# A hybrid transformer block on one core: the first modulation as fp32 matmuls in column quarters, and a written order around the first weight sums

## The chip, the cores and the metric

The kernel runs on one core of one Trainium2 chip, as one launch. Its time is device time in microseconds (us). Before the change three runs took 698.64, 700.24 and 700.47 us, with 700.24 us as their median. Five engines work side by side, each with its own queue, strictly in the order of its own instructions: PE (TensorE; its weight loads are listed as PEld), DVE (VectorE), ACT (ScalarE), POOL (GpSimd) and SP (SyncE, which here issues all transfers).

## The reference

The input x has 512 tokens of 1024 values. A vector c gives six modulation vectors, the first two of which (shift and scale) act on the first normalization. All arithmetic is fp32:

```
mod = silu(c) @ w_ada + b_ada                    # w_ada: 1024 x 6144
sh1, sc1, g1, sh2, sc2, g2 = split(mod, 6)
hn  = rms(x, norm1_g) * (1 + sc1) + sh1
y   = mixer(hn, w_in, ...)                       # three kinds of attention heads
x   = x + g1 * (y @ w_out)
hn  = rms(x, norm2_g) * (1 + sc2) + sh2
gate, up = split(hn @ w_gate_up, 2)
x   = x + g2 * ((silu(gate) * up) @ w_down)
```

The change touches two places: how sh1 and sc1 (2 x 1024 numbers, from 8 MB of w_ada) are made in the first stage, and the order of DVE and ACT where the gated part of the block (gate, up) begins.

## The kernel before, in words

**First stage.** It makes the transposed, modulated operand `hnT` (eight pieces `kc` of 128 features by 512 tokens) and, with it, one 512-column product of `w_in`, summed over the eight pieces in the four banks `gT`. Every fp32 operand of a large matmul is split into a rounded high part and the low rest (names end in h and l), and a product is three matmuls: high by high, low by high, high by low. So a step `kc` needs:

- `px_` (line 320): four 128 x 128 transposes of the scaled x on PE.
- The two modulation columns of these 128 features. w_ada lies as 8 rows k per partition; `asc` holds the scale columns and `ash` the shift columns of the piece, each 128 x 8 x 128. `scaled` (333) sums the eight rows of `asc`, times silu(c) (`cs`), on DVE into `a1`. `product` (325) multiplies six rows of `ash` on ACT and `addto` (329) sums them on POOL into `a2`; `direct` (340) multiplies the last two on PE. `colsum` (346) then sums over partitions: two matmuls with a column of ones put scale and shift as columns into `pc`. In the trace `a1` and `a2` are both called a.
- `m1_` (351, DVE) adds the constants, `hf_` (358, ACT) applies scale and shift to the transposed x, `hh_` (363) and `hl_` (369, DVE) split the result.
- `wh_` (372, ACT) and `wl_` (376, POOL) split the piece of `w_in`, and `T_` (380) does its twelve 512-column matmuls.

Before that x is squared, a reciprocal root `rs` is made by eleven tiny DVE instructions, and x is scaled (`xscale`, 300). All of these are entered with a time into a table (`ev`, 297) whose constants (PER = 3.5 us for a step, and so on) decide the order; line 423 writes them out sorted by time, and `_InOrder` (105) holds every engine to that order in this stage. The w_ada piece 0 is loaded before x.

**Where the gated part begins.** `plain(0)` and `plain(1)` (1247) are plain products of the first two column blocks for the two halves of the tokens; `plain_glu` (1264) takes their result: ACT makes `fps` = silu(gate), DVE multiplies it with up into `A`. After them the products are made by a scheme with sums of weights and operands: `sums` (1144) adds raw weight blocks r on DVE (r1t is the first such sum), ACT and DVE split it into fw16h and fw16l, and PE needs these for its first product f1A after `plain(1)`. `operand` (1073) splits operand sums (os40 among them). Temporary tiles, `fps` among them, come from `temp` (1130), a ring of 26 slots (`act_tile`, 226) that also lends a pair named sph, spl to the weights of `plain(1)`: `spare("act")` in line 1213. Here no order is imposed on DVE and ACT (line 432 has switched it off): a scheduler orders them.

Of the kernel before, what the change touches and what calls it, by code (L numbers as in the profile page):

```python
# [28 lines left out]
SHK = 6  # L29
# [102 lines left out]
def hybrid_block_kernel(  # L132
# [22 lines left out]
    def f32(ap):  # L155
        return ap.bitcast(F32)
# [103 lines left out]
    with ExitStack() as s0:  # L260
# [7 lines left out]
        for kc in range(NK):  # L268
            box["asc", kc] = ap_.tile([P, 8, P], F32, tag="asc", name=f"asc{kc}", bufs=3)
            box["ash", kc] = ap_.tile([P, 8, P], F32, tag="ash", name=f"ash{kc}", bufs=3)  # L270

        def load_ada(kc):
            SY.dma_start(box["asc", kc], w_ada_v[:, :, D + kc * P:D + kc * P + P])
            SY.dma_start(box["ash", kc], w_ada_v[:, :, kc * P:kc * P + P])

        if ADA1ST:
            load_ada(0)
# [4 lines left out]
        if not ADA1ST:  # L282
            load_ada(0)
# [11 lines left out]
        plan = []  # L295

        def ev(time, f, *a, **k):
            plan.append((time, len(plan), lambda: f(*a, **k)))

# [6 lines left out]
        for t in range(NT - 1):  # L306
            ev(XQ + 0.01 * t, square, t, slice(0, D), ss[:, t:t + 1] if t % 2 else "S")
        ssx = cp.tile([P, 1], F32, name="ssx")
        ev(XQ + 0.03, square, NT - 1, slice(0, D // 2), "S")
        ev(XQ + 0.03, square, NT - 1, slice(D // 2, D), ssx)  # L310
        ev(XQ + 0.04, V.tensor_tensor, ss[:, NT - 1:NT], ss[:, NT - 1:NT], ssx, op=ALU.add)
        ev(XR, V.tensor_scalar, v1, ss, 1.0 / D, EPS, op0=ALU.mult, op1=ALU.add)
        for i, f in enumerate(rsqrt_ops(rs, v1, "n4")):
            ev(XR + XRD * (i + 1), f)
# [10 lines left out]
        def product(kc, k):  # L325
            ash, a2 = box["ash", kc], box["a2", kc]
            S.activation(a2 if k == 0 else ash[:, k, :], ash[:, k, :], AF.Copy, scale=cs[:, k:k + 1])

        def addto(kc, k):
            ash, a2 = box["ash", kc], box["a2", kc]  # L330
            G.tensor_tensor(a2, a2, ash[:, k, :], op=ALU.add)

        def scaled(kc, k):
            asc, a1 = box["asc", kc], box["a1", kc]
            if k == 0:
                V.tensor_scalar(a1, asc[:, 0, :], cs[:, 0:1], None, op0=ALU.mult)
            else:
                V.scalar_tensor_tensor(a1, asc[:, k, :], cs[:, k:k + 1], a1, op0=ALU.mult, op1=ALU.add)

        def direct(kc):  # L340
            pc = box["pc", kc] = bank("t", f"pc{kc}")
            ash = box["ash", kc]
            for k in range(SHK, 8):
                TE.matmul(pc[:, 1:2], ash[:, k, :], cs[:, k:k + 1], start=k == SHK, stop=False)

        def colsum(kc):
            pc = box["pc", kc]
            TE.matmul(pc[:, 1:2], box["a2", kc], ones[:, 0:1], start=SHK == 8, stop=True)
            TE.matmul(pc[:, 0:1], box["a1", kc], ones[:, 0:1], start=True, stop=True)

        def m1_(kc):
            pc = box["pc", kc]
            m1 = box["m1", kc] = ap_.tile([P, 2], F32, tag="m1", name=f"m1{kc}")
            V.scalar_tensor_tensor(m1[:, 0:1], pc[:, 0:1], b1sc[:, 0, kc:kc + 1],
                                   prmT[:, 48 + kc:49 + kc], op0=ALU.add, op1=ALU.mult)
            V.tensor_tensor(m1[:, 1:2], pc[:, 1:2], prmT[:, kc:kc + 1], op=ALU.add)
# [31 lines left out]
        for kc in range(NK):  # L390
            box["a1", kc] = ap_.tile([P, P], F32, tag="a1", name=f"a1{kc}")
            box["a2", kc] = ap_.tile([P, P], F32, tag="a2", name=f"a2{kc}")
            ws = box["ws", kc] = wp.tile([P, 512], F32, tag="ws", name=f"w0s{kc}", bufs=WS)
            b_ = kc * PER
            if kc:
                ev(b_ - 9, load_ada, kc)
            ev(b_ - 9, SY.dma_start, ws, w_in[0, kc * P:(kc + 1) * P, MQK:MQK + 512])
            for k in range(8):
                ev(b_ + 0.39 * k, scaled, kc, k)
                if k < SHK:  # L400
                    ev(b_ + 0.3 * k, product, kc, k)
                    if k:
                        ev(b_ + 0.5 * k + 0.3, addto, kc, k)
            ev(b_ + TWH if kc or not ADA1ST else XQ + 0.035, wh_, kc)
            ev(b_ + TWL, wl_, kc)
            tx = max(b_ + TPX, XR + 13 * XRD, max(XT, XR + 12.5 * XRD) + XD + 0.1 if kc * P >= XS else 0)
            tc_ = b_ + TPC if kc else TPC0
            tm = tc_ + TM1 if kc else TPC0 + TM10
            th = max(tm + THF, tx + 0.1)
            ev(tx, px_, kc)  # L410
            ev(tc_, direct, kc)
            ev(tc_, colsum, kc)
            ev(tm, m1_, kc)
            ev(th, hf_, kc)
            ev(max(tm + THH, th + 0.05), hh_, kc)
            tl = max(tm + THL, th + THH - THF + 0.1)
            ev(tl, hl_, kc)
            ev(max(b_ + TPC + PER, tl) + 0.1, T_, kc)

        for i in range(NWARM):  # L420
            ev(WARM0 + WARM1 * i, TE.matmul, gT[3][:, 0:256], ident,
               box["ws", 0][:, 0:256], start=True, stop=True)
        for _, _, f in sorted(plan, key=lambda e: e[:2]):
            f()
# [875 lines left out]
    plain_glu(0)  # L1300

# [27 lines left out]
    for i, (q, ph) in enumerate(run):  # L1329
        upto = todo.index(run[min(i + AHEAD, len(run) - 1)])  # L1330
        while ahead <= upto:
            prepare(*todo[ahead])
            if todo[ahead] == (NQ - 1, 1):
                down_load(4)
            if todo[ahead] == (1, 6):
                for g_ in range(2):
                    operand("s4", g_, s4[g_])
                plain_glu(1)
            ahead += 1
        product(q, ph)  # L1340
        after(q, ph)
# [72 lines left out]
```

## Time and profile before

| | |
|---|---|
| median of three runs | 700.24 us |
| the profiled execution, its own time | 700.27 us |
| its span, first to last instruction | 698.5 us |
| PE busy | 655.9 us, 94% |
| DVE busy | 546.1 us, 78% |
| ACT busy | 370.4 us, 53% |
| POOL busy | 133.7 us, 19% |
| mean granted clock of PE | 0.98 of full |

The profile comes from one execution. Busy shares are means over stages with different limits; for a change in one stage one reads the waits and the chain of that stage. Between the span and the execution's own time lie 1.8 us in which no instruction runs. PE's clock is either at full (2.4 GHz, 1.00 in the rows) or half (1.2 GHz, 0.50); a value between is a mean over a stretch.

### The profile page before, as it was taken

The page shows a single profiled execution, that of the slowest core. Times are in us where ns is not written, and L with a number is a line of the kernel's source. Part 1 is how long each engine was busy: PE and PEld are TensorE (multiplying, and loading weights), DVE is VectorE, ACT ScalarE, POOL GpSimd, SP SyncE. Part 2 cuts the span into 40 slices and gives each one's busy share as a digit, 9 for nine tenths or more (in the row PEclk, how much of TensorE's full clock was granted, in tenths as well). Part 3 has the DMA queues.
Part 4 walks back from the last instruction along what each step waited for, and adds up shares of the span by engine and source line. Part 5 has one row for each costly group of instructions (what it writes and reads, how often), then busy time and mean ns, then how long its engine had stood idle before and what let it go on. Part 6 is the DMA issues. An engine that isn't in the chain of part 4 may idle for free.

```text
span 698.5 us, 11755 instructions
## 1 busy us (share of the span) xinstructions
PE 655.9 (94%) x4142; PEld 596.6 (85%) x4142; DVE 546.1 (78%) x1084; ACT 370.4 (53%) x757; POOL 133.7 (19%) x184
## 2 busy tenths in 40 slices
PE   2788889999999999999996999999999999999997
PEld 2677878899999998787995999999999998788885
DVE  4998978788898989978777788777778999547413
ACT  3654636557768578655852444454455575325210
POOL 5675323452442437100000000000000000000000
PEclk9999989999999999999997999999999999999999
DMA  8964683475878678630624522333332246505201
GB/s 267 284 191 101 173 197 87 132 199 159 215 188 207 180 178 233 226 94 16 209 78 150 180 61 81 104 122 121 122 121 89 69 131 198 208 6 185 82 0 61
DMA packets 95552, 99.66 MB, mean 143 GB/s; under 512 B 8187, under 2 KB 70011, under 8 KB 95493
## 3 DMA queue, kind: packets, MB, share of 16 engines
q1 hardware_dynamic: 95492, 98.91, 48.4%
q8 instruction: 33, 0.54, 0.3%
q14 instruction: 27, 0.21, 0.1%
HBM read 84.15 MB, written 2.10 MB: 123 GB/s over the span
## 4 chain that ended last, share of the span: by engine, by line
PE 66%; DVE 22%; issue 4%; ACT 3%; DMA 3%; SPq 1%; DVEq 0%; ACTq 0%
PE d L115 14%; PE F L115 6%; DVE a L115 4%; PE ol L115 4%; PE B L115 4%; PE fp L115 3%; PE mo L115 1%; DMA x<-in_x_dram 1%; PE f10A L115 1%; PE f9A L115 1%; PE f8A L115 1%; PE f7A L115 1%; PE f6A L115 1%; PE f5A L115 1%; PE f4A L115 1%
## 5 line engine op out<-in xcount | busy, mean ns | idle before, releaser
L115 ACT ACTIVATE ah<-A 128x512 fp32r<-128x512 f32 x44 | 25.6, 620 | 33.1 <-PE d L115 32.8
L115 DVE TENSOR_TENSOR al<-A,ah 128x512 fp32r<-128x512 f32 x44 | 29.1, 687 | 17.8 <-ACT ah L115 17.8
L115 DVE SCALAR_TENSOR_TENSOR a<-asc,cs,a 128x128 f32<-128x128 f32 x56 | 29.8, 532 | 1.4
L115 POOL TENSOR_TENSOR a<-a,ash 128x128 f32<-128x128 f32 x40 | 23.9, 598 | 14.8 <-ACT ash L115 12.3
L115 DVE TENSOR_TENSOR r<-r,r 128x1024 f32<-128x1024 f32 x20 | 24.4, 1221 | 0.3
L115 DVE TENSOR_TENSOR fo<-d,g1b 128x512 f32<-128x512 f32 (+1 forms) x9 | 5.6, 631 | 17.9 <-PE d L115 17.8
L115 ACT ACTIVATE Fp<-Fs,Fmn 128x128 f32<-128x128 f32 (+3 forms) x24 | 12.6, 527 | 11.1 <-DVE Fmn L115 7.1
L115 POOL TENSOR_SCALAR Fp<-Fp,Fls 128x128 f32<-128x128 f32 (+2 forms) x18 | 12.3, 683 | 27.3 <-DVE Fls L115 18.2
L115 ACT ACTIVATE Bp<-Bs,Bmn 128x128 f32<-128x128 f32 (+3 forms) x24 | 12.6, 526 | 6.9 <-DVE Bmn L115 4.1
L115 PE MATMUL pc<-ones,a 128*128 128x1 f32 x32 | 5.9, 267 | 10.4 <-POOL a L115 5.8
L115 POOL TENSOR_SCALAR Bp<-Bp,Bls 128x128 f32<-128x128 f32 (+2 forms) x16 | 8.7, 543 | 35.0 <-DVE Bls L115 25.1
L115 ACT ACTIVATE hf<-px,m 128x512 f32<-128x512 f32 x8 | 6.2, 776 | 17.3 <-DVE m L115 13.5
L115 PEld LDWEIGHTS pc<-ones,a 128*128 128x128 f32 x32 | 5.0, 206 | 11.0 <-POOL a L115 6.0
L115 ACT ACTIVATE u<-u 128x512 f32<-128x512 f32 x20 | 12.5, 626 | 3.4 <-DVE u L115 3.4
L115 DVE TENSOR_TENSOR A<-u,u 128x512 f32<-128x512 f32 x20 | 13.7, 686 | 0.0
L115 ACT ACTIVATE smh<-E 128x512 fp32r<-128x512 f32 (+3 forms) x16 | 7.5, 470 | 11.0 <-DVE E L115 10.9
L115 DVE CUSTOM_DVE_ANT_0 Bs<-Bs,mask 128x128 f32<-128x128 f32 (+3 forms) x24 | 11.6, 492 | 2.0 <-PE Bs L115 2.0
L115 POOL TENSOR_TENSOR sml<-E,smh 128x512 fp32r<-128x512 f32 (+1 forms) x8 | 8.8, 1101 | 22.3 <-ACT smh L115 22.3
L115 DVE TENSOR_TENSOR Bptl<-Bpt,Bpth 128x128 fp32r<-128x128 f32 (+3 forms) x24 | 11.5, 485 | 1.7 <-ACT Bpth L115 1.5
L115 ACT ACTIVATE Fpth<-Fpt 128x128 fp32r<-128x128 f32 (+3 forms) x24 | 10.5, 436 | 4.5 <-PE Fpt L115 4.4
L115 ACT ACTIVATE ash<-ash,cs 128x128 f32<-128x128 f32 x40 | 12.7, 389 | 0.0
L115 DVE CUSTOM_DVE_ANT_0 Fs<-Fs,mask 128x128 f32<-128x128 f32 (+3 forms) x24 | 11.7, 489 | 1.0 <-PE Fs L115 1.0
(2328 smaller groups left out, 2874.3 us busy)
## 6 DMA issues: line engine op xcount, KB each, us to landing
r<-in_w_gate_up_dram SPq DMA_DIRECT2D x40, 512.0 KB, 4.7
dr<-in_w_down_dram SPq DMA_DIRECT2D x22, 512.0 KB, 5.2
asc<-in_w_ada_dram SPq DMA_DIRECT2D x8, 512.0 KB, 5.6
ash<-in_w_ada_dram SPq DMA_DIRECT2D x8, 512.0 KB, 7.5
x<-in_x_dram SPq DMA_DIRECT2D x4, 512.0 KB, 8.7
w0s<-in_w_in_dram SPq DMA_DIRECT2D x8, 256.0 KB, 7.1
g10s<-in_w_ada_dram SPq DMA_DIRECT2D x8, 256.0 KB, 3.8
g11s<-in_w_ada_dram SPq DMA_DIRECT2D x8, 256.0 KB, 2.9
```

Of the source, the lines that this page charges most:

```text
L115: r = f(*a, **k)
```

## The change

**First stage.** The table of times is gone: the code is written in the order in which each engine is to work. x is loaded first, then the pieces of w_ada (both halves in one tile `ada`, 128 x 8 x 2 x 128, five buffers) and of `w_in`. For a piece, `mv_` does eight fp32 matmuls: the stationary operand is one column of `cs`, repeated 32 times, the moving one a row of `ada` with 256 columns; row k goes to the quarter k % 4 of the array's columns and to the 32 partitions of `pc` that belong to it, so that each quarter sums two rows. ACT copies the 128 x 256 result, divided by 32, to `row`, and `colsum` adds over the partitions as before. `asc`, `ash`, `a1`, `a2` and their work on DVE, ACT and POOL are gone, and `wl_` has moved from POOL to DVE. `T_` is cut in two: four matmuls before `colsum`, eight behind it.

**Where the gated part begins.** From `plain_glu(0)` on, DVE and ACT are held to the written order, up to the preparation of product (1, 7); the operand sums `s4` and `plain_glu(1)` are written behind that one, instead of behind (1, 6).

```
-SHK = 6
+ADB = 5
...
+        def load_kc(kc):
+            a_ = box["ada", kc] = ap_.tile([P, 8, 2, P], F32, tag="ada", name=f"ada{kc}", bufs=ADB)
+            for i in range(2):
+                SY.dma_start(a_[:, :, i, :], w_ada_v[:, :, i * D + kc * P:i * D + kc * P + P])
+            ws = box["ws", kc] = wp.tile([P, 512], F32, tag="ws", name=f"w0s{kc}", bufs=WS)
+            SY.dma_start(ws, w_in[0, kc * P:(kc + 1) * P, MQK:MQK + 512])
...
-        if not ADA1ST:
-            load_ada(0)
+        for kc in range(ADB - 1):
+            load_kc(kc)
...
+        for i in range(NWARM):
+            TE.matmul(gT[3][:, 0:256], ident, sq[2][:, 0:256], start=True, stop=True)
...
-        def product(kc, k):
-            ash, a2 = box["ash", kc], box["a2", kc]
-            S.activation(a2 if k == 0 else ash[:, k, :], ash[:, k, :], AF.Copy, scale=cs[:, k:k + 1])
...
-        def direct(kc):
+        def mv_(kc):
             pc = box["pc", kc] = bank("t", f"pc{kc}")
+            a_ = box["ada", kc].rearrange("p k i n -> p k (i n)")
+            for k in range(8):
+                g_ = k % 4
+                TE.matmul(pc[32 * g_:32 * g_ + 32, 0:256], cs[:, k:k + 1].to_broadcast([P, 32]), a_[:, k, :],
+                          start=k < 4, stop=k >= 4)
+            r_ = box["row", kc] = ap_.tile([P, 2, P], F32, tag="row", name=f"row{kc}")
+            S.activation(r_.rearrange("p i n -> p (i n)"), pc[:, 0:256], AF.Copy, scale=1.0 / 32)

         def colsum(kc):
             pc = box["pc", kc]
-            TE.matmul(pc[:, 1:2], box["a2", kc], ones[:, 0:1], start=SHK == 8, stop=True)
-            TE.matmul(pc[:, 0:1], box["a1", kc], ones[:, 0:1], start=True, stop=True)
+            for i in range(2):
+                TE.matmul(pc[:, 256 + i:257 + i], box["row", kc][:, i, :], ones[:, 0:1], start=True, stop=True)
...
-            (G if kc in WLG else V).tensor_tensor(l_, box["ws", kc], f32(box["wh", kc]), op=ALU.subtract)
+            V.tensor_tensor(l_, box["ws", kc], f32(box["wh", kc]), op=ALU.subtract)
...
+        px_(0)
         for kc in range(NK):
+            mv_(kc)
+            wh_(kc)
             if kc:
+                T_(kc - 1, (0,))
+            colsum(kc)
+            m1_(kc)
+            wl_(kc)
+            hf_(kc)
+            hh_(kc)
+            hl_(kc)
+            if kc == 0:
+                for t in range(NT):
+                    xscale(t, XS, D)
+            else:
+                T_(kc - 1, (1, 2))
+            if kc + 1 < NK:
+                px_(kc + 1)
+            if kc + ADB - 1 < NK:
+                load_kc(kc + ADB - 1)
+        T_(NK - 1, (0, 1, 2))
...
     plain_glu(0)
+    in_order["V"][0] = in_order["S"][0] = 1
...
-            if todo[ahead] == (1, 6):
+            if todo[ahead] == (1, 7):
                 for g_ in range(2):
                     operand("s4", g_, s4[g_])
                 plain_glu(1)
+                in_order["V"][0] = in_order["S"][0] = 0
```

DVE in the first stage, around pieces 4 and 5, before: a is the running sum, m the modulation column, hn the split operand.

```order
L115 TENSOR_TENSOR m_509<-pc_484,prmT 128x1
L115 SCALAR_TENSOR_TENSOR a_194<-asc_151,cs,a_194 128x128 x4
L115 CAST hn4h<-hf_516 128x512
L115 TENSOR_SCALAR a_197<-asc_153,cs 128x128
L115 SCALAR_TENSOR_TENSOR a_197<-asc_153,cs,a_197 128x128
L115 TENSOR_TENSOR hn4l<-hf_516,hn4h 128x512
L115 SCALAR_TENSOR_TENSOR a_197<-asc_153,cs,a_197 128x128 x2
L115 SCALAR_TENSOR_TENSOR m_561<-pc_536,b1sc,prmT 128x1
```

DVE at the same place, after:

```order
L115 SCALAR_TENSOR_TENSOR m_409<-pc_390,b1sc,prmT 128x1
L115 TENSOR_TENSOR m_409<-pc_390,prmT 128x1
L115 TENSOR_TENSOR w0l_412<-w0s_250,w0h_401 128x512
L115 CAST hn4h<-hf_414 128x512
L115 TENSOR_TENSOR hn4l<-hf_414,hn4h 128x512
```

The eight sums of a step have left DVE's queue, and the low part of the weights, w0l, has come into it.

PE in the first stage, from the transposes of one piece on, before (gT 171 to 174 are the four banks):

```order
L115 MATMUL px_628<-ident,x_165 128x128
L115 MATMUL pc_636<-cs,ash_156 128x1 x2
L115 MATMUL pc_636<-ones,a_201 128x1
L115 MATMUL pc_636<-ones,a_200 128x1
L115 MATMUL gT_171<-hn6h,w0h_565 128x512
```

PE there, after (gT 173 to 176 are the banks):

```order
L115 MATMUL px_467<-ident,x_147 128x128
L115 MATMUL pc_472<-ada_339,cs 32x256 x8
L115 MATMUL gT_173<-hn5h,w0h_442 128x512
L115 MATMUL gT_174<-hn5h,w0h_442 128x512
L115 MATMUL gT_175<-hn5h,w0h_442 128x512
L115 MATMUL gT_176<-hn5h,w0h_442 128x512
L115 MATMUL pc_472<-ones,row_481 128x1 x2
L115 MATMUL gT_173<-hn5h,w0l_453 128x512
```

Eight matmuls of 32 x 256 have come in ahead of the product of the piece before, and the two column sums stand behind its first four matmuls.

ACT where the gated part begins, with its waits, before (fps0 and fps1 belong to the two `plain_glu`):

```order
L115 ACTIVATE os31h_4966<-hf11_4662 128x512
L115 ACTIVATE os40h_5016<-s40_4964 128x512 [waits DVE_49,PE_49]
L115 ACTIVATE fps0_4999<-fp00_4724 128x512 [waits DVE_49]
L115 ACTIVATE os41h_5020<-s41_4970 128x512 [waits PE_49]
L115 ACTIVATE fps1_5024<-fp10_4838 128x512 [waits DVE_49,PE_49]
L115 ACTIVATE fw16h_5012<-r1t_4989 128x1024 [waits DVE_49]
```

ACT there, after:

```order
L115 ACTIVATE os31h_4854<-hf11_4550 128x512
L115 ACTIVATE fps0_4887<-fp00_4612 128x512 [waits PE_49,Activation_49]
L115 ACTIVATE fw16h_4900<-r1t_4877 128x1024 [waits DVE_49,Activation_49]
L115 ACTIVATE fw15h_4904<-r100_4879 128x1024
L115 ACTIVATE fw17h_4909<-r101_4881 128x1024 [waits DVE_49]
L115 ACTIVATE os40h_4913<-s40_4852 128x512
L115 ACTIVATE fw14h_4951<-r110_4885 128x1024
L115 ACTIVATE os41h_4917<-s41_4858 128x512
L115 ACTIVATE fps1_4921<-fp10_4726 128x512 [waits PE_49]
```

os40h, os41h and fps1 have gone behind the first weight splits; fps0 now stands directly ahead of them. In the built program of before, fps0 takes the ring slot of s40. In that of after it takes the slot of sph, and its wait on PE names the second last matmul of `plain(1)`, the last one that reads sph.

## Rows read from the trace of the kernel before

**Rows 1.** Chain that ended last, 24.8 to 67.1 us, its shares by line.

```profile
by line: DVE a L115 60.2%; PE gT L115 16.3%; DVE x L115 2.9%; DVE m L115 2.8%; DVE hn6h L115 2.2%; issue 1.8%; DVE hn1l L115 1.4%; DVE hn4l L115 1.4%; DVE hn0l L115 1.4%; DVE hn3l L115 1.4%; DVE hn5l L115 1.4%; DVE hn2l L115 1.4%; DVE hn1h 
```

**Rows 2.** Stretches: us, busy PE, PEld, DVE, ACT, POOL; clock, DMA share, GB/s.

```profile
31.50:37.34 5.84, 4.38 (x25) 3.69 (x25) 5.66 (x13) 3.48 (x9) 4.83 (x8) 1.00 0.76 229
59.80:64.03 4.23, 4.22 (x12) 3.35 (x13) 4.05 (x9) 1.09 (x2) 1.31 (x5) 0.60 0.49 101
64.03:67.13 3.10, 3.10 (x14) 2.25 (x12) 0.46 (x2) 1.07 (x3) 2.83 (x5) 1.00 0.51 120
```

**Rows 3.** Groups, 24.8 to 67.1 us: busy us, mean ns | idle before, releaser.

```profile
L115 DVE SCALAR_TENSOR_TENSOR a<-asc,cs,a 128x128 f32<-128x128 f32 x42 | 24.0, 571 | 1.0
L115 ACT ACTIVATE hf<-px,m 128x512 f32<-128x512 f32 x7 | 5.4, 778 | 17.3 <-DVE m L115 13.5 <-PE pc L115 3.8
```

**Rows 4.** PE in time, steps 6 and 8: start us, us, instruction.

```profile
56.79 0.60 PE L115 MATMUL px<-ident,x 128*128 128x128 f32 x4
57.22 0.50 PE L115 MATMUL pc<-cs,ash 128*128 128x1 f32 x4
57.59 0.36 PE L115 MATMUL pc<-ones,a 128*128 128x1 f32 x2
...
64.25 1.07 PE L115 MATMUL gT<-hn7h,w0h 128*128 128x512 f32 x4
65.16 1.07 PE L115 MATMUL gT<-hn7h,w0l 128*128 128x512 f32 x4
```

**Rows 5.** A plain fp32 matmul with 512 columns (tile g1p), its two records.

```profile
134.02 1.02 PE L115 MATMUL g1p<-g,ones 128*128 128x512 f32 x2
...
L115 PE MATMUL g1p<-g,ones x4: 592/592/592, 134.0 to 164.9; 128*128 128x512 f32 x4
```

**Rows 6.** DVE, ACT and PE in time, from the start to the first product.

```profile
6.79 0.28 DVE L115 TENSOR_SCALAR a<-asc,cs 128x128 f32<-128x128 f32 x1 [3.03 <-DMA asc<-in_w_ada_dram]
...
11.88 1.23 DVE L115 CUSTOM_DVE_ANT_0 sq<-x 128x1024 f32<-128x1024 f32 x1 [2.02 <-DMA x<-in_x_dram]
...
14.61 0.69 DVE L115 CUSTOM_DVE_ANT_0 sq<-x 128x512 f32<-128x512 f32 x1 [1.49 <-DMA x<-in_x_dram]
...
15.24 4.91 PE L115 MATMUL gT<-w0s,ident 128*128 128x256 f32 x12 [0.76 <-DMA w0s<-in_w_in_dram]
...
16.01 1.21 DVE L115 TENSOR_SCALAR rs<-n4s 128x4 int32<-128x4 int32 x1
17.25 0.16 DVE L115 SCALAR_TENSOR_TENSOR n4a<-rs,v 128x4 f32<-128x4 f32 x1
...
19.12 1.11 ACT L115 ACTIVATE x<-x,rs 128x384 f32<-128x384 f32 x2
...
24.79 1.19 PE L115 MATMUL gT<-hn0h,w0h 128*128 128x512 f32 x4 [0.95 <-DVE hn0h L115]
```

**Rows 7.** PE in time: ten array columns (pR), then 64 array rows (ms<-Q).

```profile
97.58 0.52 PE L115 MATMUL F<-F0w4h,hn4h 128*128 128x384 f32 x1
97.90 1.05 PE L115 MATMUL pR<-ident,ar 128*10 128x128 f32 x4
...
99.08 0.52 PE L115 MATMUL F<-F0w4h,hn4l 128*128 128x384 f32 x1
...
99.85 0.69 PE L115 MATMUL ms<-Q,K 64*128 64x384 f32 x1
```

**Rows 8.** ACT, DVE and PE in time, where the gated part begins.

```profile
371.64 0.69 DVE L115 TENSOR_TENSOR A<-fp,fps 128x512 f32<-128x512 f32 x1 [3.96 <-PE fp L115]
...
374.64 1.22 DVE L115 TENSOR_TENSOR r1t<-r,r 128x1024 f32<-128x1024 f32 x1
...
375.89 1.06 ACT L115 ACTIVATE fw16h<-r1t 128x1024 fp32r<-128x1024 f32 x1 [5.16 <-DVE r1t L115]
...
377.00 0.58 PE L115 MATMUL f1A<-os20h,fw16h 128*128 128x256 f32 x1 [5.47 <-ACT fw16h L115]
...
378.05 1.22 DVE L115 TENSOR_TENSOR fw16l<-r1t,fw16h 128x1024 fp32r<-128x1024 f32 x1
```

More of the change, by code (lines that the diff above doesn't have):

```diff
@@ L267, in hybrid_block_kernel @@
         box = {}
[L268 to L276, printed above, removed]
-            load_ada(0)
+        def load_kc(kc):
[4 more added lines that the diff above has]
+            SY.dma_start(ws, w_in[0, kc * P:(kc + 1) * P, MQK:MQK + 512])
         for t in range(NT):
@@ L281, in hybrid_block_kernel @@
             xt.append(xx)
-        if not ADA1ST:
-            load_ada(0)
+        for kc in range(ADB - 1):
+            load_kc(kc)
         sq = [ap_.tile([P, D], F32, tag=f"sq{t % 2}", name=f"sq{t}", bufs=1) for t in range(NT)]
@@ L294, in hybrid_block_kernel @@
         gT = [bank("g", f"gT{m}") for m in range(4)]
-        plan = []
-        def ev(time, f, *a, **k):
-            plan.append((time, len(plan), lambda: f(*a, **k)))
         def xscale(t, c0, c1):
@@ L306, in hybrid_block_kernel @@
         for t in range(NT - 1):
-            ev(XQ + 0.01 * t, square, t, slice(0, D), ss[:, t:t + 1] if t % 2 else "S")
+            square(t, slice(0, D), ss[:, t:t + 1] if t % 2 else "S")
         ssx = cp.tile([P, 1], F32, name="ssx")
[L309 to L314, printed above, removed]
+        square(NT - 1, slice(0, D // 2), "S")
+        square(NT - 1, slice(D // 2, D), ssx)
+        V.tensor_tensor(ss[:, NT - 1:NT], ss[:, NT - 1:NT], ssx, op=ALU.add)
+        V.tensor_scalar(v1, ss, 1.0 / D, EPS, op0=ALU.mult, op1=ALU.add)
+        for f in rsqrt_ops(rs, v1, "n4"):
+            f()
+        for i in range(NWARM):
+            TE.matmul(gT[3][:, 0:256], ident, sq[2][:, 0:256], start=True, stop=True)
         for t in range(NT):
-            ev(XR + 12 * XRD, xscale, t, 0, XS)
-        for t in range(NT):
-            ev(max(XT, XR + 12.5 * XRD) + t // 2 * XD, xscale, t, XS, D)
+            xscale(t, 0, XS)
         def px_(kc):
@@ L353, in m1_ @@
             m1 = box["m1", kc] = ap_.tile([P, 2], F32, tag="m1", name=f"m1{kc}")
-            V.scalar_tensor_tensor(m1[:, 0:1], pc[:, 0:1], b1sc[:, 0, kc:kc + 1],
+            V.scalar_tensor_tensor(m1[:, 0:1], pc[:, 257:258], b1sc[:, 0, kc:kc + 1],
                                    prmT[:, 48 + kc:49 + kc], op0=ALU.add, op1=ALU.mult)
-            V.tensor_tensor(m1[:, 1:2], pc[:, 1:2], prmT[:, kc:kc + 1], op=ALU.add)
+            V.tensor_tensor(m1[:, 1:2], pc[:, 256:257], prmT[:, kc:kc + 1], op=ALU.add)
         def hf_(kc):
@@ L377, in wl_, with T_ @@
             l_ = box["wl", kc] = wp.tile([P, 512], F32R, tag="wl", name=f"w0l{kc}")
-            (G if kc in WLG else V).tensor_tensor(l_, box["ws", kc], f32(box["wh", kc]), op=ALU.subtract)
-        def T_(kc):
+            V.tensor_tensor(l_, box["ws", kc], f32(box["wh", kc]), op=ALU.subtract)
+        def T_(kc, parts):
             hh, hl = hnT[kc]
             wh, wl = box["wh", kc], box["wl", kc]
-            for w_, h_ in ((wh, hh), (wl, hh), (wh, hl)):
+            for i in parts:
+                w_, h_ = ((wh, hh), (wl, hh), (wh, hl))[i]
@@ L384, in T_ @@
                 for m in range(4):
-                    TE.matmul(gT[m], w_[:, m * P:(m + 1) * P], h_, start=kc == 0 and w_ is wh and h_ is hh,
-                              stop=kc == NK - 1 and h_ is hl)
+                    TE.matmul(gT[m], w_[:, m * P:(m + 1) * P], h_, start=kc == 0 and i == 0,
+                              stop=kc == NK - 1 and i == 2)
+        px_(0)
         for kc in range(NK):
-            box["a1", kc] = ap_.tile([P, P], F32, tag="a1", name=f"a1{kc}")
-            box["a2", kc] = ap_.tile([P, P], F32, tag="a2", name=f"a2{kc}")
@@ L393, in hybrid_block_kernel @@
-            ws = box["ws", kc] = wp.tile([P, 512], F32, tag="ws", name=f"w0s{kc}", bufs=WS)
-            b_ = kc * PER
+            mv_(kc)
+            wh_(kc)
             if kc:
[L396 to L424, printed above, removed]
+                T_(kc - 1, (0,))
+            colsum(kc)
+            m1_(kc)
```

12 lines of the change are left out of this document (removed).

## The prediction

> **What bounds the kernel now.** I read three views, in this order. First the chain of waits for the first stage, from its first product (24.8 us) to its last (67.1 us): the reader is to see that 60% of it is one DVE line, the running sum a, and PE's own matmuls 16% [rows 1]. Then the same stage by stretches and by groups: in a typical step of 5.84 us DVE is busy for 5.66 us and PE for 4.38 us [rows 2], and the 42 sums take 571 ns each, while ACT's hf waited 13.5 us in total for the DVE column m behind them [rows 3]. So the stage is paced by DVE, not by PE and not by its loads. Behind it comes a kernel in which PE is busy nearly all the time, so I let what the stage gains arrive at the end in full. Last the one large hole of PE later on: 5.47 us at 371.5 us, ended by fw16h, which waited for the DVE sum r1t [rows 8].
>
> **The loads.** Today the first 512 KB piece of w_ada is usable at 6.79 us, and the last two steps of x come 2.73 us apart (11.88 and 14.61 us), 1.37 us a tile [rows 6]. With x first I put its first tile at the 6.7 us of today's first transfer and the fourth at 6.7 + 3 x 1.37 = 10.8 us, 3.8 us earlier. From there to the scaled x it is 14.61 to 20.23 us today (ACT's 19.12 + 1.11); one tiny instruction in between took 1.21 us where the next took 0.16 [rows 6], while POOL worked. POOL has nothing to do there any more, so I take 1.05 us off: 10.8 + 5.62 - 1.05 = 15.4 us. The six warming matmuls (4.91 us) now need only the square of the third tile, and end about there too. The first piece `ada` comes after x, two tiles of 1.37 us: 13.5 us, and even at twice the price (16.3 us) it would come about when it is needed.
>
> **The price of the eight new matmuls.** No row shows fp32 matmuls in several column quarters, so I bound them. A plain fp32 matmul has two records; 512 columns show 1.02 us for two records of 0.592 us, so a record occupies PE for 0.43 us and lets go 0.16 us later [rows 5]. At 256 columns that is 0.214 us a pass, and eight matmuls have 16 passes.
> - All in turn: 16 x 0.214 = 3.42 us.
> - Four quarters fully side by side: two rounds of two passes, 0.86 us.
> - Between them: PE takes its queue in order, and the second pass of a quarter must follow its first. Then the first pass of the next quarter can run beside that second pass, but no earlier: 9 slots, 1.93 us.
>
> I take 1.93 us. It is the only one of the three that needs both that quarters run side by side and that the queue stays in order, and every row has starts in order.
>
> A change of form may cost something too. Ten-column matmuls (pR) stand in the trace between full ones: the one before them started 0.32 us ahead, and the next unhidden full one 1.18 us after the first of them, which is four passes of 0.21 us (1.05 us less the last record's 0.42, over three) and 0.32 us. Nothing was lost [rows 7]. With 64 array rows instead, ms<-Q starts 0.13 us later than two times 0.32 us after 99.08, and its record is 0.17 us longer than the 0.52 us of its neighbours [rows 7]. pR has the form of the new matmuls (all rows, at most 32 columns), so I take nothing; 0.3 us at each of 16 changes would be 4.8 us. The Trainium skill (TensorEngine Tiling (Array Packing), Tiling Modes) says that changing the tiling mode drains TensorE, which speaks against this change; pR does not show it for columns, ms<-Q does for rows. By that rule and ms<-Q's price the sum would be 4.8 us higher.
>
> **The first stage added up.** PE pieces at full clock: the twelve matmuls of T take 3 x 0.91 = 2.72 us, the four transposes 0.43, the two column sums 0.37 (as the two small matmuls that they follow) [rows 4]. Piece 0 goes through in a chain: transposes from 15.4 to 15.85, matmuls to 17.8, release and ACT's copy (half of hf's 0.78 us [rows 3] for half the columns) to 18.4, column sums to 18.8, transposes of piece 1 to 19.2, its matmuls to 21.15. By then m, hf and hh of piece 0 are done: 2.36 us have gone since the column sums, and hf, the longest of the three, takes 0.78. So the first product starts at 21.15 us instead of 24.79 [rows 6]. From there PE has 8 x 2.72 + 6 x 0.43 + 7 x 0.37 + 6 x 1.93 = 38.5 us, and ends at 59.7, with its last record at 59.9 us. Today the end is at 67.13 us [rows 2]. **-7.2 us.**
>
> What I count at nothing: `wl_` on DVE (its new queue has five short instructions a step, where it had thirteen) and the copies `row` (four matmuls of T, 0.91 us, cover release and copy, 0.55 us; without that cover 8 x 0.5 us). The loads of later pieces: SP issues four pieces ahead, and a piece is 1.25 MB, 3.4 tiles of 1.37 us, so 4.7 us a step against PE's 5.45; at the price of the first piece it would be PE's pace and no more, so a bound of 2 us the wrong way. SP's queue: behind the loads stand the weights of the next stage, which wait for the same splits as today. DVE's queue near the end has a third accumulate for g1 ahead of the last hn; it waits for its load, and it is work that is gone later: I set one against the other.
>
> **The written order at 371 us.** It looks like the end of the 5.47 us hole: the sums no longer stand behind the second A. But fps0 stands ahead of fw16h on ACT, and the first A ahead of the sums on DVE; and fps0 got the slot of sph, which `plain(1)` reads until its second last matmul. So ACT stands at fps0 until about 371.5 us. Then: fps0 0.6 us, A 0.6 us, the sum r100 1.13, r1t from 373.95 instead of 374.64, fw16h at 375.2 instead of 375.89; fw16l, behind only four sums where five stood, at 377.3 instead of 378.05 [rows 8]. Gain 0.7 us; some of it goes because fw17 and fw14 now come behind other work, and PE meets fw14h earlier. **-0.4 us**; from -2 to +1.5, as clock and new waits fall. If fps0 did not wait, the hole would go: another -5.5 us and the time at half clock behind it, some 2.5 us.
>
> Sum: -7.6 us. The profiled execution took 700.27 us (the median of the three is 700.24, the same within a hundredth of a per cent), so **692.7 us**; with the bounds of form changes, loads and order 689.5 to 697.5.
>
> **The rivals.**
> - *Quarters in turn.* Then 1.49 us more for each of eight pieces: +11.9, 704.6 us, slower than before. The place is `mv_` on PE, and it decides from 2.88 us a piece on (7.6 / 8 more than 1.93). For it: 16 passes are all PE rows that a plain matmul would have, and no row shows two at once. Against it: pR lets full matmuls follow it without a drain, so a part of the array seems to be held by itself.
> - *Four side by side.* 0.86 us a piece. The first product then waits for hh, at about 19.4 us, and 32.2 us follow: the stage ends at 51.8, 684.6 us in all. For it: quarters share no weights and no result partitions. Against it: the two passes of a quarter stand together in the queue. The Trainium skill (TensorE: Matmul & The Clock Gate, Part 3) has three column tiles 2.38 times as fast as in turn; at that rate four tiles would take an estimated 1.08 us a piece, some 686 us. No row here shows it.
> - *The clock falls as it does now.* Three T's of today ran at a mean like that of the stretch from 59.80 us, 0.60 of full clock and 4.23 us for twelve matmuls [rows 2]; each time PE had stood waiting or done only tiny matmuls ahead of them. The new stage has no such gaps, but a quarter of the array may not keep the clock up. Three such T's again: 3 x 1.5 = +4.5, 697.2 us; more would be no gain.
> - *The order does what it says* would give 684.7 us with my first stage; the slot speaks against it, and I give it no more than 2 in 100, counted with the second rival.
>
> **How the numbers follow.** My forecast 0.50, in turn 0.22, side by side (with the last one) 0.14, falling clock 0.14. A run of this kernel tells changes over 0.3% (2.1 us) from none: faster is below 698.2 us. Faster: 0.48 of the forecast, 0.14, and 0.06 of the third, 0.68. Slower: the first, and 0.01 of the third, 0.23. Same: 0.09. The range for 8 in 10 goes from 685 to 705: it leaves out the lower half of the second rival and nearly half of the first.
>
> **What would show it.** The first product (gT<-hn0h) near 21 us and the last near 60; eight matmuls of 32 x 256 in 1.9 us, with starts of about 0.21 us; DVE no longer in the chain between; clock at 1.00 there. At 371 us fps must still wait for PE. I am wrong if mv_ takes over 2.9 us, if T waits for a load, if PE's clock falls between 21 and 60 us, or if f1A starts before 374 us.

## The result, and the profile after

The changed kernel takes 692.24 us (median of four runs, 691.67 to 693.40), the kernel before 699.66 us in the same count: ratio 0.9897, 95% interval 0.9876 to 0.9918. The forecast was 692.7 us. The number was met, but two steps of the sum failed by about the same amount in opposite directions, so that it was met by luck in good part; most of the experiments below are about these two. The profiled execution of the changed kernel is the slowest of the four, 693.40 us (span 691.4).

The first stage came out 3.6 us better than forecast. Stretches of the kernel after (us, busy PE, PEld, DVE, ACT, POOL; granted clock, DMA share, GB/s): one step of the first stage, the start of the next stage, three more stretches of that one, and one behind the plain products.

```profile
24.41:29.29 4.88, 4.88 (x40) 3.54 (x36) 2.00 (x5) 1.68 (x3) 0.00 (x0) 1.00 1.18 306
56.30:68.70 12.40, 12.39 (x97) 12.20 (x96) 12.32 (x16) 8.41 (x16) 7.13 (x7) 1.00 0.60 167
71.60:75.50 3.90, 3.90 (x13) 3.90 (x14) 3.62 (x14) 3.88 (x11) 1.28 (x1) 0.56 0.42 98
84.81:92.50 7.69, 7.68 (x30) 6.51 (x31) 2.54 (x9) 0.01 (x1) 0.00 (x0) 0.56 0.53 118
98.60:102.30 3.70, 3.70 (x12) 3.15 (x13) 1.82 (x6) 1.51 (x5) 1.28 (x1) 0.55 0.00 0
...
369.00:376.00 7.00, 5.53 (x24) 5.03 (x24) 7.00 (x7) 3.39 (x5) 0.00 (x0) 0.54 0.48 137
```

Against the step of before in [rows 2] DVE's 5.66 us of 5.84 have become 2.00 of 4.88, and PE has no gap: PE paces the stage now. PE in time (start us, us, instruction, in brackets the idle time before it and what ended it):

```profile
18.55 1.07 PE L115 MATMUL pc<-ada,cs 128*32 128x256 f32 x16 [0.59 <-DMA ada<-in_w_ada_dram]
19.55 1.19 PE L115 MATMUL gT<-hn0h,w0h 128*128 128x512 f32 x4
...
22.88 0.60 PE L115 MATMUL px<-ident,x 128*128 128x128 f32 x4
23.41 1.07 PE L115 MATMUL pc<-ada,cs 128*32 128x256 f32 x16
24.41 1.21 PE L115 MATMUL gT<-hn1h,w0h 128*128 128x512 f32 x4
25.46 0.50 PE L115 MATMUL pc<-ones,row 128*128 128x1 f32 x4
25.83 1.17 PE L115 MATMUL gT<-hn1h,w0l 128*128 128x512 f32 x4
26.84 1.09 PE L115 MATMUL gT<-hn1l,w0h 128*128 128x512 f32 x4
27.76 0.60 PE L115 MATMUL px<-ident,x 128*128 128x128 f32 x4
...
53.29 1.19 PE L115 MATMUL gT<-hn7h,w0h 128*128 128x512 f32 x4 [1.08 <-DVE hn7h L115]
...
55.23 1.07 PE L115 MATMUL gT<-hn7l,w0h 128*128 128x512 f32 x4
...
71.60 0.59 PE L115 MATMUL F<-F0w0h,hn0h 128*128 128x384 f32 x1 [2.88 <-DVE Vm L115]
...
84.81 0.61 PE L115 MATMUL pF<-gtmp,tri 128*128 128x10 f32 x4 [2.03 <-DVE gtmp L115]
...
369.00 0.58 PE L115 MATMUL f1A<-os20h,fw16h 128*128 128x256 f32 x1 [4.90 <-ACT fw16h L115]
...
371.25 0.58 PE L115 MATMUL f1A<-os20h,fw16l 128*128 128x256 f32 x1 [1.46 <-DVE fw16l L115]
```

The sixteen passes of a piece take 1.00 us (23.41 to 24.41). The first product starts at 19.55 us and the last ends at 56.3, where before they stood at 24.79 [rows 6] and 67.13 us [rows 2]: 10.8 us gained. The span is only 7.1 us shorter. The missing 3.7 us go in the next stage, whose products are called F and pF. There DVE takes Vm out of the banks of the products A before the first F starts, and makes gtmp for pF in a chain of tiny instructions, the gate chain. Two rows of before:

```profile
81.43 0.41 PE L115 MATMUL F<-F0w0h,hn0h 128*128 128x384 f32 x1 [1.86 <-DVE Vm L115]
...
93.79 0.61 PE L115 MATMUL pF<-gtmp,tri 128*128 128x10 f32 x4 [2.05 <-DVE gtmp L115]
```

At the first F product the lead is 9.8 us (81.43 to 71.60), at pF 9.0 (93.79 to 84.81), at the first F1 product 7.0 (111.39 to 104.36); from there to 371 us it stays between 7.0 and 7.9. PE waits there for DVE, and three stretches of half clock follow, of which before had only the one behind pF in this stage (0.55 from 93.79 to 101.00 us). In the two that are new, the first of half clock and the third, the clock is 0.56 and 0.55: of 3.90 and 3.70 us 1.7 each are lost to it.

How much is lost there differs from execution to execution. Kernels e3, e4 and e5 below are the same as after up to 350 us. Up to pF, where DVE sets the time, they lose 1.8 to 1.9 us of the lead, as after does. From pF to the first F1 product after loses another 2.0 us, e5 0.6 and e4 0.1, and e3 gains 0.5; in e3 and e4 the third stretch of half clock did not come. A row of e3:

```profile
94.00:106.00 12.00, 11.83 (x61) 9.35 (x60) 10.01 (x25) 9.12 (x32) 3.40 (x4) 1.00 0.31 84
```

So of the 3.7 us some 1.8 were lost in every one of these executions, and the rest came and went with the clock.

ACT and DVE of the kernel after, at three places that matter below:

```profile
13.85 1.12 ACT L115 ACTIVATE x<-x,rs 128x384 f32<-128x384 f32 x2 [2.71 <-DVE rs L115]
...
79.73 1.00 DVE L115 TENSOR_TENSOR F0w7l<-F0w7s,F0w7h 128x384 fp32r<-128x384 f32 x1 [1.29 <-ACT F0w7h L115]
...
364.08 0.60 ACT L115 ACTIVATE fps<-fp 128x512 f32<-128x512 f32 x1 [12.05 <-PE fp L115]
367.89 1.06 ACT L115 ACTIVATE fw16h<-r1t 128x1024 fp32r<-128x1024 f32 x1 [3.21 <-DVE r1t L115]
```

### The profile page after: what moved, and what is told of

The parts are those of the page before. It is cut to its first block, busy times and chain, and to the rows that moved or that the text cites. A ratio compares the mean times of both kernels' runs of the same rounds, so it can differ in the third digit from the quotient of the medians.

```text
span 691.4 us, 11769 instructions
## 1 busy us (share of the span) xinstructions
PE 656.2 (95%) x4238; PEld 593.0 (86%) x4238; DVE 518.6 (75%) x1028; ACT 359.3 (52%) x717; POOL 101.0 (15%) x136
## 4 chain that ended last, share of the span: by engine, by line
PE 73%; DVE 15%; DMA 4%; issue 4%; ACT 3%; SPq 2%; DVEq 0%; ACTq 0%
PE d L115 14%; PE F L115 7%; PE B L115 6%; PE fp L115 3%; PE ol L115 3%; PE gT L115 2%; SPq L115 2%; PE mo L115 1%; PE f9A L115 1%; PE f8A L115 1%; PE f7A L115 1%; PE f6A L115 1%; PE f5A L115 1%; PE f4A L115 1%; PE f3A L115 1%
## 5 line engine op out<-in xcount | busy, mean ns | idle before, releaser
L115 DVE SCALAR_TENSOR_TENSOR m<-pc,b1sc,prmT 128x1 f32<-128x1 f32 x8 | 1.7, 218 | 18.5 <-PE pc L115 18.5
L115 PE MATMUL gT<-sq,ident 128*128 128x256 f32 x12 | 4.4, 546 | 10.4 <-ACT sq L115 10.4
L115 PEld LDWEIGHTS gT<-sq,ident 128*128 128x128 f32 x12 | 3.4, 291 | 11.0 <-issue 10.3
L115 PE MATMUL Bpt<-ident,Bp 128*128 128x128 f32 x60 | 10.8, 277 | 1.7 <-DVE Fyp L115 0.7
L115 DVE TENSOR_TENSOR Fptl<-Fpt,Fpth 128x128 fp32r<-128x128 f32 (+3 forms) x24 | 11.6, 483 | 0.6 <-ACT Fpth L115 0.4
L115 ACT ACTIVATE Bpth<-Bpt 128x128 fp32r<-128x128 f32 (+3 forms) x24 | 10.3, 433 | 3.2 <-PE Bpt L115 2.8
```

Source lines behind the costliest of these rows:

```text
L115: r = f(*a, **k)
```

## The experiments

Times are medians; "before" is the same kernel of before on the same chip. Each is an edit of the kernel after, unless it says otherwise.

**Full width (e1).** The eight matmuls go through all 128 columns of the array.

```
-                g_ = k % 4
-                TE.matmul(pc[32 * g_:32 * g_ + 32, 0:256], cs[:, k:k + 1].to_broadcast([P, 32]), a_[:, k, :],
-                          start=k < 4, stop=k >= 4)
+                TE.matmul(pc[:, 0:256], cs[:, k:k + 1].to_broadcast([P, P]), a_[:, k, :],
+                          start=k == 0, stop=k == 7)
...
```

> The eight fp32 matmuls of a piece go through the whole width of the array instead of four quarters: same rows, same 256 columns, one sum of eight, scale 1/128. In the trace of after, the sixteen passes of a piece take 1.00 us from the first start to the start of the next matmul. Theory A (passes of different quarters really run at the same time, four in the time of one): here 16 x 0.214 = 3.42 us a piece, 2.42 more, and the last product of the stage ends 8 x 2.42 = 19.4 us later than after's 56.3, near 75.7; if the stage's loss arrives at the end in full, 692.2 + 19.4 = 711.6 us; if the following stage gives back a part, as it took 3.8 us of the stage's gain, 704 to 711. Theory B (256-column fp32 matmuls are simply cheaper than the long ones suggest, the quarters do little): under 1.5 us a piece, and 692 to 696 us.

Measured 708.38 us (706.59 to 710.21), ratio 1.0126 (1.0102 to 1.0151): slower than before. PE, one piece:

```profile
35.29 3.62 PE L115 MATMUL pc<-ada,cs 128*128 128x256 f32 x16
38.55 1.28 PE L115 MATMUL gT<-hn2h,w0h 128*128 128x512 f32 x4
```

3.26 us a piece against 1.00: theory A. The same sixteen passes cost three times as much when they cannot share the array, and with that price the change makes the kernel slower instead of faster. The stage ends 18.2 us later, the kernel 16.1.

**Two halves (e9).** 64 columns instead of 32, row k to half k % 2 (one run).

> As after, but two halves of 64 columns instead of four quarters of 32 (row k to half k % 2, scale 1/64). Theory (what runs at once is set by the number of column parts): eight rounds of 0.196 to 0.22 us, 1.65 us a piece, between after's 1.00 and the full width's 3.27; the stage ends 8 x 0.65 = 5 us later than after's.

```profile
36.97 1.95 PE L115 MATMUL pc<-ada,cs 128*64 128x256 f32 x16
38.85 1.20 PE L115 MATMUL gT<-hn3h,w0h 128*128 128x512 f32 x4
```

1.88 us a piece, more than the 1.65 expected, and 698.11 us; the stage ends 7.8 us later than after's. Full width, halves and quarters stand as 3.26, 1.88, 1.00: the number of parts sets the price. Behind the first, the single passes of one part start 0.216 us apart in all three kernels; sixteen, eight and four such rounds are 3.45, 1.73 and 0.86 us. So halves and quarters have about 0.15 us beside their rounds, and at full width the next product starts sooner behind the last pass.

**The order of the rows (e2).** The two rows of a quarter stand next to each other in the queue: `g_ = k // 2`, start and stop with k % 2.

> Four quarters as in after, but the two rows of a quarter stand next to each other in PE's queue (row k goes to quarter k // 2). Theory A (the forecast's: PE takes its queue in order, a pass waits for the one ahead): four passes of a quarter in turn, and only the last one of a quarter beside the first of the next: 13 slots of 0.214 us, 2.8 us a piece, stage 8 x 1.8 = 14 us longer, 700 to 707 us. Theory B (each quarter works off its own matmuls while PE goes on handing out): as after, 1.0 us a piece, 692 us. Something between tells how many matmuls of a quarter can be waiting while the others start.

Measured 693.28 us (692.59 to 694.35), ratio 0.9911 (0.9894 to 0.9929), not told from after.

```profile
38.24 1.09 PE L115 MATMUL pc<-ada,cs 128*32 128x256 f32 x16
39.26 1.20 PE L115 MATMUL gT<-hn4h,w0h 128*128 128x512 f32 x4
```

1.02 us a piece: theory B. The step of the forecast that let the next quarter start only beside a second pass is refuted where it should have shown most, with four passes of a quarter in a row. The single passes say the same: in either kernel four of them have started within 0.05 us of the first, and the fifth starts 0.24 us after it. What has started by 23.44 us in after, and by 23.66 us here:

```profile
23.41 0.42 PE L115 MATMUL pc<-ada,cs 128*32 128x256 f32 x4
```

```profile
23.61 0.44 PE L115 MATMUL pc<-ada,cs 128*32 128x256 f32 x4
```

So the order of PE's queue, which I called strict, is not kept between passes of different quarters.

**Loads in the old order (e7).** `load_kc(0)` ahead of x.

> As after, but the first piece of w_ada (512 KB twice 256 KB apart) and of w_in are loaded ahead of x, as before the change. Theory A (the load order brought part of the earlier start): x comes 1.25 MB later, 3.4 tiles of 1.37 us, so the first product gT<-hn0h starts at 22 to 24 us instead of 19.6, and the total is 2.5 to 4 us longer: 695 to 696. Theory B (loads bound the stage up to 45 us whatever their order): first product later, last product of the stage and total unchanged.

Measured 695.38 us (694.63 to 697.01), ratio 0.9943 (0.9922 to 0.9963): 3.1 us more than after. PE's first product:

```profile
23.24 1.19 PE L115 MATMUL gT<-hn0h,w0h 128*128 128x512 f32 x4 [0.24 <-DVE hn0h L115]
```

3.7 us later than after's 19.55, and the stage ends 4.3 us later: theory A. So nearly half of the whole gain is lost when the old load order is put back.

**Without the written order at 371 us (e3).** `in_order` and the place of `s4` and `plain_glu(1)` as before the change.

> The first stage of after, but the gated part as before the change (no written order on DVE and ACT, operand sums and the second silu behind product (1, 6)). Theory A (forecast: the order gains 0.4 us): 692.6 us, hole of 5.5 us, first f1A 0.6 us later against the end of the plain products. Theory B (what aligning the two traces says: the order starts f1A 0.58 us earlier and gives back 0.8 us by product f1C): 692.0 us, all of it in the first half microsecond of difference that a timing can't resolve. More than 1 us either way refutes both.

Measured 691.32 us (690.57 to 692.43), ratio 0.9883 (0.9866 to 0.9901), which overlaps after's interval.

```profile
368.00 0.58 PE L115 MATMUL f1A<-os20h,fw16h 128*128 128x256 f32 x1 [5.46 <-ACT fw16h L115]
```

The hole is before's [rows 8] again, and the time no longer; the two theories lie too near each other for these times to choose between them. The second half of the change is worth nothing that can be measured, and the traces speak against it: from the plain products to product f2A this kernel gains 1.0 us on after.

**The gate written into A (e4).** silu(gate) goes into A itself, so no ring slot is taken.

```
-        t_ = temp(f"fps{hb}")
-        S.activation(t_, g_, AF.Silu)
...
+        t_ = ffn["A"][0][:, :, 256 * hb:256 * hb + 256]
+        S.activation(t_, g_.rearrange("p (a b) -> p a b", a=2), AF.Silu)
...
```

> Written order as in after, but silu(gate) is written straight into A and multiplied there, so it no longer takes the ring slot of sph and needs only the end of plain(0). Theory A (the slot alone makes the hole of 4.90 us, and the half clock comes from the hole): fw16h is ready long before plain(1) ends, hole and half clock go, some 8 us less: 684 us. Theory B (the next wait takes its place: DVE has the sum r200 ahead of fw16l, and the load of its second operand is issued only when plain(1) ends, 362.7 us in after): the first two products of f1A start at once, the third waits for fw16l until about 370 us, 691.5 us.

Measured 690.37 us (689.63 to 692.51), ratio 0.9874 (0.9847 to 0.9900): theory B. DVE, then PE:

```profile
365.61 1.23 DVE L115 TENSOR_TENSOR r<-r,r 128x1024 f32<-128x1024 f32 x1 [8.60 <-DMA r<-in_w_gate_up_dram]
...
369.16 0.58 PE L115 MATMUL f1A<-os20h,fw16l 128*128 128x256 f32 x1 [5.53 <-DVE fw16l L115]
```

The hole of 4.90 us has moved two matmuls on and is 5.53 us: DVE stands 8.60 us at a sum whose load has not come, with fw16l behind it. The 1.9 us under after lie within what the two intervals share; in the traces this kernel gains 2.0 us on after at this place.

**The sums in order too (e5).** As the last one, and the written order holds until product (2, 6) is prepared, so that this sum stands behind the first splits.

```
                 plain_glu(1)
+            if todo[ahead] == (2, 6):
                 in_order["V"][0] = in_order["S"][0] = 0
```

> As e4 (gate straight into A), and the written order of DVE and ACT holds until product (2, 6) is prepared, so the sum r200, which waits for a load that is issued only when plain(1) ends, stands behind the first weight splits instead of ahead of fw16l. In e4 PE waited 5.53 us for fw16l, and DVE stood 8.60 us at r200. Theory A (that load was the last wait): fw16l is ready near 359 us, the hole and the half clock behind it go: 5.5 + 0.7 us of waits and some 2.5 us of half clock less than e4's 690.4, about 682. Theory B (a further wait of the same size takes over: os40h, fw17 or the operands of product (2, 6)): 688 to 690.

Measured 683.03 us (682.73 to 683.96), ratio 0.9765 (0.9748 to 0.9783): theory A.

```profile
362.00:368.00 6.00, 6.00 (x52) 6.00 (x52) 4.16 (x5) 3.89 (x6) 0.00 (x0) 1.00 0.79 251
368.00:374.00 6.00, 6.00 (x52) 6.00 (x52) 3.40 (x4) 1.86 (x3) 0.00 (x0) 1.00 1.10 350
```

PE is busy throughout at full clock, where in after it had a hole and then 0.54. The time is 9.2 us under after's, of which the slot alone gave 1.9; the longer written order alone was not run. In the traces the lead over after is 0.5 us at 360 us and 10.1 behind 390, so the gain is made at this place.

**One tap (e6).** Each convolution leaves out two of its three shifted products, so DVE has eight instructions less between the two stages.

> As after, but each of the four convolutions adds one of its three shifted products on DVE (the other two are left out): 8 DVE instructions of 0.7 to 1.2 us less between the first stage and the first F product. Theory A (the 3 to 4 us that the first stage gained and the end did not see were lost because DVE, fully busy from 50 to 72 us, paces the next stage): PE's wait of 2.88 us for Vm shrinks below 1 us, and the total falls by 2 to 5 us, to 687 to 690. Theory B (lost to the half clock alone, or to loads): the wait for Vm goes down but PE's pace behind does not change, total within 1 us of 692.2.

Measured 686.64 us (685.75 to 686.85), ratio 0.9811 (0.9791 to 0.9831). PE in time, then its stretch behind pF:

```profile
72.53 0.41 PE L115 MATMUL F<-F0w0h,hn0h 128*128 128x384 f32 x1 [3.10 <-DVE Vm L115]
...
80.43 0.51 PE L115 MATMUL pF<-gtmp,tri 128*128 128x10 f32 x4
...
80.43:88.00 7.57, 7.57 (x46) 6.41 (x46) 4.85 (x11) 2.61 (x5) 1.81 (x2) 1.00 0.32 89
```

The total is theory A's, 5.6 us less; its place is not. The wait for Vm is as long as it was: in the room that the missing products left, DVE does sums for g and splits ahead of Vm. What went is the wait for gtmp: pF starts at 80.43 instead of 84.81 us, and F0w7l, the low part of a weight split that in after stands in DVE's queue ahead of ten of the gate chain's instructions, stands behind the chain here. The clock behind pF is 1.00 where after had 0.56.

**F0w7l on POOL (e8).** As e5, with that one split moved to POOL.

> As e5, and the low part of the weights F0w7 is made by POOL instead of DVE. In after DVE stands 1.29 us at F0w7l, which waits for ACT's F0w7h and that for its load, and runs it for 1.00 us, with the chain of tiny gate instructions (gtmp) behind it; PE then waits 2.03 us for gtmp and goes on at half clock. In e6, where F0w7l happened to stand behind the gate chain, pF started 4.3 us earlier than in after. Theory A (this place in DVE's queue costs a part of what the first stage gained): pF starts 2 to 3 us earlier than e5's 85.7, its wait goes, total 2 to 3 us less than e5's 683.0: 680 to 681. Theory B (the DVE work as a whole is what costs, e6 gained by its missing instructions): pF under 1 us earlier, 682.5 to 683.5.

Measured 679.75 us (679.25 to 682.44), ratio 0.9726 (0.9702 to 0.9751). The total is just below theory A's, but pF moved by 0.96 us only, which is theory B's. PE of e5; then of this kernel the group of DVE between 78 and 86 us, the same instructions from 80.03 to 84.1 us alone, and POOL and PE in time:

```profile
85.66 0.61 PE L115 MATMUL pF<-gtmp,tri 128*128 128x10 f32 x4 [2.11 <-DVE gtmp L115]
```

```profile
L115 DVE SCALAR_TENSOR_TENSOR gtmp<-gtmp 128x40 f32<-128x40 f32 x9 | 5.0, 560 | 0.3
...
L115 DVE SCALAR_TENSOR_TENSOR gtmp<-gtmp 128x40 f32<-128x40 f32 x4 | 4.0, 1010 | 0.1
...
80.93 1.00 POOL L115 TENSOR_TENSOR F0w7l<-F0w7s,F0w7h 128x384 fp32r<-128x384 f32 x1
...
84.70 0.61 PE L115 MATMUL pF<-gtmp,tri 128*128 128x10 f32 x4 [1.63 <-DVE gtmp L115]
```

Matched matmul by matmul, this kernel is 1.0 us ahead of e5 at pF and 3.0 us at the first F1 product; PE ran at half clock for some 7 us between 70 and 102 us here, and for some 10 us in e5.

**F0w7l behind the gates (e10).** As e5, the split stays on DVE, held behind the last gate instruction by a dependency without a semaphore.

> As e5, F0w7l stays on DVE but is held behind the last gate instruction (pre), so POOL gets no new work. In e8 the nine gate instructions took 5.32 us, against 3.10 in after, while POOL ran three splits and a low part beside them, and pF started only 0.96 us earlier than in e5. Theory A (DVE's place and POOL's work are two separate costs): the nine take 3.1 us again, and the chain is rid of the wait of 1.29 and of F0w7l, so pF starts 2 to 2.5 us earlier than e5's 85.7 and 1 us earlier than e8's 84.7; total 1.5 to 3 us under e5's 683.0. Theory B (the nine wait for POOL whenever they come): they take over 4.5 us, pF 84.5 or later, total within 1 us of e5's or e8's.

Measured 676.56 us (675.35 to 679.44), ratio 0.9668 (0.9655 to 0.9682), the fastest version. The same group, then DVE, POOL and PE in time:

```profile
L115 DVE SCALAR_TENSOR_TENSOR gtmp<-gtmp 128x40 f32<-128x40 f32 x9 | 1.8, 199 | 0.3
...
82.69 1.28 DVE L115 TENSOR_TENSOR pre<-gtmp 128x10 f32<-128x10 f32 x1
82.68 1.26 POOL L115 TENSOR_TENSOR mql<-qkz,mqh 128x512 fp32r<-128x512 f32 x1 [2.64 <-ACT mqh L115]
...
82.76 0.56 PE L115 MATMUL pF<-gtmp,tri 128*128 128x10 f32 x4
```

pF starts 2.9 us earlier than in e5, without a wait. Theory A holds for the place, DVE's order there. The nine did not meet POOL, which stands idle from 80.05 to 82.68 us while they run; so the cost that e8 shows was avoided here, not disproved. The total fell by 6.5 us, more than the 1.5 to 3 expected (3.9 us between the two profiled executions; this kernel's is the slowest of its five). From 92 to 100 us PE was busy 6.64 us at a clock of 0.86 in e5, and is 7.53 us at 1.00 here. This stretch and an earlier one of e5 with the wait ahead of it, then of e10:

```profile
72.35 0.41 PE L115 MATMUL F<-F0w0h,hn0h 128*128 128x384 f32 x1 [2.72 <-DVE Vm L115]
...
72.40:76.40 4.00, 4.00 (x17) 4.00 (x18) 3.73 (x14) 3.98 (x11) 1.27 (x1) 0.68 0.48 111
92.00:100.00 8.00, 6.64 (x31) 5.45 (x30) 6.64 (x13) 5.27 (x15) 2.17 (x2) 0.86 0.67 173
```

```profile
72.68 0.41 PE L115 MATMUL F<-F0w0h,hn0h 128*128 128x384 f32 x1 [2.71 <-DVE Vm L115]
...
72.40:76.40 4.00, 3.72 (x22) 3.75 (x23) 3.73 (x15) 3.98 (x11) 1.29 (x1) 1.00 0.49 109
92.00:100.00 8.00, 7.53 (x39) 5.96 (x39) 6.00 (x17) 5.82 (x21) 1.40 (x2) 1.00 0.72 190
```

So a part of it is the clock, which no longer falls at either place. At the first F product e10 is 0.3 us behind e5; at 76 us, still ahead of the gate chain, it is 1.3 us ahead, because the clock has stayed up; at pF it is 2.9 and at the first F1 product 4.4 us ahead. So of what e10 gains in the traces a good half is the clock, ahead of the chain and behind it, and the chain's own part is some 1.6 us. The mean clock over the span is 0.996 to 0.997 in all five executions of e10 and 0.990 to 0.992 in those of e5, so this is no accident of the profiled ones; why the clock stays up is open.

## Why the prediction was right, and where it was not

**What bounds the kernel: right.** DVE's running sums paced the first stage; with them gone PE paces it.

**The loads: right.** The scaled x was put at 15.4 us and was there at 14.97 (13.85 + 1.12). The second piece of w_ada held PE for 0.59 us, against nothing in the sum.

**The price of the eight matmuls: wrong, and the largest error.** The step that failed is that the first pass of the next quarter can run beside a quarter's second pass "but no earlier", and with it the nine slots and 1.93 us. Measured: 1.00 us, the second rival's 0.86, which is four rounds of 0.216 us, and 0.14 beside them. None of the rows I read the queue's order from shows matmuls of different quarters side by side; they could not tell whether a pass waits for the queue or only for its own part of the array. Rows adjacent in one quarter cost the same, so it is the part. The price of the rival of quarters in turn is that of full width, 3.26 measured against 3.42. The rule in the Trainium skill (TensorE: Matmul & The Clock Gate, Part 3) pointed the right way: it has three column tiles 2.38 times as fast as in turn, and here four were 3.26 times and two 1.73 times as fast as full width. The estimate of 1.08 us a piece that the prediction draws from it was a better guide than my reading of rows that did not bear on it.

**The other pieces of PE: a little too cheap.** The twelve matmuls of T take 1.05, 1.01 and 0.92 us, 2.98 instead of 2.72; the first four after another form cost 0.1 us more each time. The transposes take 0.53, not 0.43. With 0.37 for the column sums a step is 4.88 us where 5.45 was forecast and 4.38 by the second rival. The Trainium skill (TensorEngine Tiling (Array Packing), Tiling Modes) has a drain at a change of mode. The rows here leave room for 0.14 us in the 1.00, 0.1 in the transposes ahead and 0.1 in the first four matmuls behind, 0.34 us a piece and 2.7 us in eight, if all of it is the drain, which no run shows. I had counted nothing and named 4.8 us as its price.

**The stage: -10.8 us, not -7.2.** The first product came 1.6 us earlier than forecast (two pieces stand ahead of it), the end 3.6 us earlier. Not counted was the wait of 1.08 us for hn7h at the end. The accumulate that I had weighed there stands behind hn7l in DVE's queue and does not hold it up; instead the low part w0l of that piece took 1.03 us and the split hn7h 0.97, where the other pieces have 0.68 and 0.43, 0.9 us more together, each with a split of POOL's running beside it (50.28 to 51.05 and 51.91 to 52.95 us).

**"Let what the stage gains arrive at the end in full": wrong.** This is the second failed step, and it took back 3.7 us in the profiled execution. I read that PE is busy nearly all the time later and did not look at the stage right behind: there DVE is busy all the time (12.32 of 12.40 us from 56.30 on), so an earlier start of PE only meets it earlier. e6, e8 and e10 point to the place, DVE's queue around the gate chain, and to the half clock behind PE's waits as the other part of the price. Delays do not arrive in full either: e1, e9 and e7 end the stage 18.2, 7.8 and 4.3 us later than after and the kernel 16.1, 5.9 and 3.1.

**The order at 371 us: right in its mechanism.** fps waited for PE until 364.08 us, the hole shrank from 5.47 to 4.90 us (0.57 where 0.7 was forecast), and it was given back: the next products met fw16l (1.46 us) and half clock, and the lead over the trace of before was 7.4 us at the last plain product, 8.0 at the first f1A and 7.2 from product f2A on. So in the traces the forecast of -0.4 us for this part has the wrong sign, by less than the times can tell. What I put down for the hole without the slot's wait, 5.5 + 2.5 us, was about the right size (9.2 with e5), but not the slot's alone: behind it waited a load.

**The clock: right.** At 1.00 in the whole first stage; the rival of the falling clock did not come there, but it came one stage later.

**One of the signs of being wrong.** The sign "if f1A starts before 374 us" came by its letter: f1A started at 369.00. The bound was written in the times of before and left out the first stage's own gain; with 7.4 us of lead 369.00 is 376.4 there, and PE did wait for fw16h.

So the sum is -10.8 + 3.7 = -7.1 us in the two profiled executions and -7.4 in the medians, where -7.2 - 0.4 = -7.6 was forecast. The stage gave 3.6 us more than forecast, and behind it 3.7 us went where another 0.4 was to come. That the two nearly cancelled is luck; what was right is that DVE's sums set the pace, that PE sets it without them, and the loads.

## What to carry to other kernels

Small fp32 matmuls with few output rows were worth spreading over the column quarters here, in either order in the queue; price them at the passes of one quarter plus 0.1 to 0.3 us, not at a queue's slots. When a stage is shortened, read the stage behind it before adding the gain to the end: if another engine is full there, look at that engine's order and at the clock behind PE's waits. And when a wait is taken away, look in the queue of the engine behind it for the next instruction that waits for something later still; the first edit here (e4) was worth 1.9 us alone, the second on top of it (e5) 7.3.

## What the runs showed of the hardware that was not expected

**POOL holds DVE up.** The nine gate instructions take 199 ns each where POOL is quiet (e10). Where it works beside them (e8) the mean is 560 ns: four of the nine, one beside each of POOL's four instructions, take 1010 ns in the mean, and the other five 0.20 us. `pre`, of ten columns, took 1.28 us from 82.69 us on in e10: POOL's `mql` started at 82.68 and took 1.26. A tiny DVE instruction with two operands then lasts until POOL's has ended. The Trainium skill (SBUF — State Buffer, SBUF: two separate sides) has the pair of ports that the two engines share as a lock held for the whole instruction, and these rows agree. Moving work to POOL was thus little relief for a chain of tiny DVE instructions: pF came 0.96 us earlier in e8.

**The clock's price.** In the kernel after, PE's waits of 2.88 us at 71.6 and of 2.03 us at 84.8 are each followed by a stretch with a mean clock of 0.56, which costs 1.7 us of 3.90 and 3.4 us of 7.69: in the second case more than the wait. Whether the clock falls differed after the same wait for Vm: behind 2.72 us of it the mean from 72.40 to 76.40 us was 0.68 in e5, behind 2.71 us 1.00 in e10. Why is open.
